# Six weight blocks kept on chip, an earlier load in the v task, other PSUM tiles for two gate blocks, and 384 tokens in token layout

## The chip, the cores and the metric

One core of a Trainium2 chip runs the whole kernel. The metric is the device time of one execution in microseconds (us); lower is better. The core has TensorE (PE, matmuls and transposes into PSUM), VectorE (DVE), ScalarE (ACT), GpSimd (POOL) and SyncE (SP). SP and ACT issue the DMAs. PEld in the profile is PE's weight loading, and a name with q behind it (SPq, ACTq) is an engine's instruction queue.

## The reference

One inference step through two layers for 1024 prompt tokens and 32 sample tokens, width 1024, all in float32.

```python
# layer 0 (even): a | u v | gate = rms_norm(x) @ w_in (1024 x 5120)
y_a = pool_mixer(a, ...)                 # trailing means 2/4/8/16 minus a, per-group linear, scale
u, v = gelu(uv);  v = layer_norm(v)      # for the sample tokens v is an output (state_sgu_v_sample)
y_b = u * (W_s v + b)                    # chunks of 128 positions, 4 heads, chunk-causal
x = x + rms_norm((concat(y_a, y_b) * silu(gate)) @ w_out)
# layer 1 (odd): q_c (384) | kv_c (256) | k_r (64) | gate (1024) = rms_norm(x) @ w_in_odd
q = rms_norm(q_c) @ w_q_up;  ckv = rms_norm(kv_c);  k_rope, q_rope = rope(...)
o = softmax(mask((q_abs . ckv + q_rope . k_rope) * scale)) @ ckv      # 8 heads
x = x + rms_norm((o @ w_kv_up_v * silu(gate)) @ w_o)
```

Outputs are x of both groups, the pool and v states, and the key caches.

## The kernel before, in words

Activations lie transposed, 128 channels by 1056 tokens (1024 prompt, 32 sample). Tokens are cut in part "a" (columns 0 to 639, two matmuls of 320) and part "b" (640 to 1055, one of 416). Every float32 operand is split in a high and a low half (`float32r`), and a product is three matmuls: high x high, high x low, low x high. `prep_w` (L140) fetches a weight block of 128 x 1024 in two halves of 512 columns: a DMA on SP into `raw` (three buffers), a cast on ACT to `whi` (four buffers), and the difference on POOL, or on DVE where `lo_on` says so, to `wlo` (four buffers). `mm_block` (L164) multiplies one block.

PE's instructions stand in the order in which the program writes them. A small planner writes them: `mm` adds each matmul's estimated time to a clock `now`, `spawn` puts a task (a Python generator) in a list with a due time, `poll` after each k step lets one due task write its next piece, and each `yield` says how long to wait, from the table `N` (ns). `drain` writes out all that is left. The instructions of DVE, ACT, POOL and the DMA queues are put in order by the compiler, which may move an instruction ahead of others where its inputs are there, by its own estimate; on the chip each engine then keeps that order. The compiler also adds the waits, and a tile's place is taken over when the last user of the tile before it is done.

Layer 0 (`even`, L319): blocks 8 and 9 (u) are accumulated while x arrives, "a" in the PSUM tiles `zt[0]` and `zt[1]`, "b" in the two halves (two banks) of `zt[2]`. Then come the gate blocks 32 and 33, part by part, and `evac` (L188) multiplies each result by the norm. `t_prep` (L374) makes sums and differences of x; with them 14 pairs of blocks run as seven products each (`pair_block`, L468) in the three tiles of `zt` by turns, their weights loaded by `s_load` (L424) and split by `s_prep` (L446, L447). Pairs 0 to 3 are v. `v_task` (L540) transposes each on PE and writes it to DRAM (`vd`); after pair 3 `lead_task` (L510) reads `vd` back by 128 tokens in nine steps, into R(15) and R(12) by turns, takes mean and variance (L518 to L522), normalises (L523) and writes `vnd`. For the 32 sample tokens it applies gain and shift in two halves and writes the output.

Between the layers `residual` (L863) adds x and the normed output, for "a" and "b", splits the new x for layer 1 (L895, L896), and sums the squares for the next norm (L907); `rstd` (L200) makes the norm's row from such a sum: L209 on PE, L216 to L219, L227, then L240.

Layer 1: `odd_in` (L911) multiplies w2. Its first six blocks run for "a", then again for "b", because the norm of "b" comes later; `seq` lists them twice and `prep_w` fetches them each time. Eight gate blocks follow for "ab". Attention (L1032) writes `ogd`. The last product (`output`, L1277) is cut by tokens: the first 2 x OA columns, here 800, in eight blocks with the weights stationary (matmuls of 400, tag "za" of PSUM, here `sc`), the other 256 in token layout, two tiles of 128 tokens with the tokens stationary and 512 output channels moving (`tile_k`, L1339). `turn` (L1326) transposes these tokens' x. `final_a` (L1372) norms and writes the first part while the token tiles run: two DVE instructions per block (L1385, L1386). Each token tile ends with squares on ACT (L1361), the product with the gain (L1362), the power on POOL (L1366), L1369 and the write. PSUM has here two `sc` tiles of two banks and four `pj` banks, and "zb" and "mi" stand for `pj`.

Of the kernel before, what the change touches and what calls it, by code (L numbers as in the profile page):

```python
# [24 lines left out]
OA = 400  # L25
# [9 lines left out]
N = {"ld0": 18000, "ld": 8500, "tp": 5500, "sa": 9000, "sl": 12000, "sb": 6000, "sbk": 2000, "sg": 0, "x": 462, "mix": 3200, "mixq": 2450, "tr": 717, "lead": 9000, "tr0": 11989, "res": 9194, "ra": 2699,  # L35
# [41 lines left out]
class Build:  # L77
# [62 lines left out]
    def prep_w(self, src, n=1024, lo_on=None, pool=None):  # L140
# [3 lines left out]
        for o in range(0, n, 512):  # L144
            m = min(512, n - o)
            raw = self.t(self.stg, [P, 512], F32, "raw", bufs=RAW)
            hi = self.t(pool or self.stg, [P, 512], F32R, "whi", bufs=4)
            lo = self.t(pool or self.stg, [P, 512], F32R, "wlo", bufs=4)
            nc.sync.dma_start(raw[:, :m], src[:, o : o + m])
            nc.scalar.copy(hi[:, :m], raw[:, :m])  # L150
            (lo_on or nc.gpsimd).tensor_tensor(lo[:, :m], raw[:, :m], hi[:, :m], ALU.subtract)  # L151
            res.append((hi, lo))
# [166 lines left out]
    def even(self):  # L319
# [91 lines left out]
        wts[33] = self.prep_w(self.i_w1[33], lo_on=nc.vector)  # L411
# [75 lines left out]
        for g, z in (("a", zz), ("b", z)):  # L487
# [5 lines left out]
            for i in range(2):  # L493
                ps = (zt[i], None) if g == "a" else (None, zt[2][:, i, :])
# [15 lines left out]
        def lead_task():  # L510

            for t in range(9):
                n = P if t < 8 else 32
                v = R(12 if t % 2 else 15)[:n, :D]
                nc.sync.dma_start(v, vd[t, :n])
                bs = self.t(evc, [P, 2, 6], F32, "bs", bufs=2)
# [8 lines left out]
                if t == 8:  # L525
                    w = R(13)
                    for e in range(2):
                        lg, lnb = w[:32, :512], w[:32, 512:1024]
                        o = slice(e * 512, e * 512 + 512)
                        nc.sync.dma_start(lg, self.i_lnbc[:, o])  # L530
                        nc.sync.dma_start(lnb, self.i_lnbc[:, D + e * 512 : D + e * 512 + 512])
                        nc.vector.tensor_tensor(lg, lg, v[:, o], ALU.mult)
                        nc.vector.tensor_tensor(lg, lg, lnb, ALU.add)
                        nc.scalar.dma_start(self.o_sv[:, o], lg)
# [26 lines left out]
        for p, (b0, b1) in enumerate(pairs):  # L561
# [6 lines left out]
            if p < 4:  # L568
                self.spawn(v_task(p, d), N["tr0"])
# [293 lines left out]
    def residual(self, g, acc, y):  # L863
# [47 lines left out]
    def odd_in(self):  # L911
        nc = self.nc
        h2 = self.h2
        wts = {0: self.prep_w(self.i_w2[0])}
        seq = list(range(6)) * 2 + list(range(6, 14))
        z = self.yp[:6]

        def block(i, groups, ps=None):
            w = wts.pop(i)
            if i + 1 < len(seq):  # L920
                wts[i + 1] = self.prep_w(self.i_w2[seq[i + 1]])
            return self.mm_block(self.wcol(w), h2, range(NK), groups, ps=ps)
# [3 lines left out]
        for b in range(6):  # L926
            pss.append(block(b, "a"))
# [12 lines left out]
        pss = [block(6 + b, "b", (None, zs[b])) for b in range(4)]  # L940
        self.drain()
        for b in range(6):
            self.evac(pss[b] if b < 4 else block(6 + b, "b"), z[b], rep2, "b")
# [73 lines left out]
        for m in range(8):  # L1017
            ps = block(12 + m, "ab")
# [258 lines left out]
    def output(self, w2, z2):  # L1277
# [59 lines left out]
        z = [self.bank("za") for _ in range(nt)]  # L1337

        def tile_k(j, k):  # L1339
            xh, xl = (v.b[:, j * P : (j + 1) * P] for v in og[k])  # L1340
            for c in range(2):
                hi, lo = wr[k][c]
                for e, (xx, w) in enumerate(((xh, hi), (xh, lo), (xl, hi))):
                    self.mm(z[j][:, c, :], xx, w, k == 0 and e == 0, k == NK - 1 and e == 2, 512)
# [7 lines left out]
        for j in range(nt):  # L1352
# [6 lines left out]
            for c in range(2):  # L1359
                junk = self.t(tp, [P, na], F32, "a", bufs=2)  # L1360
                nc.scalar.activation(junk[:, :512], z[j][:, c, :], AF.Square, accum_out=st[:, c : c + 1])  # L1361
            nc.vector.tensor_tensor(yg.rearrange("p (c n) -> p c n", c=2), z[j],  # L1362
                                    gb.rearrange("p (c n) -> p c n", c=2), ALU.mult)
# [124 lines left out]
```

## Time and profile before

| | |
|---|---|
| median of 3 runs | 1305.01 us (1299.88, 1305.31, 1305.01) |
| the profiled execution | 1299.84 us, span 1298.0 us |
| mean granted PE clock | 0.991 of full speed |
| busy: PE, DVE, ACT, POOL | 1255.4, 862.1, 552.5, 306.4 us |
| HBM read and written | 101.74 and 36.21 MB |

The page shows busy times, the chain of work that ended last, and groups of instructions by line. The waits view names for each idle time the engine, the line that waited, and what released it. A row of the windows view gives a stretch, the busy us of PE, PEld, DVE, ACT and POOL with their instruction counts, then the granted clock, the DMA share and GB/s. A timeline row is start, duration, engine, line, operation, output <- input, shape and count; in brackets stands the idle time before it and what ended that. Some 28 us of PE's span are idle by the timeline, the last 13.94 us aside.

### The profile page before, as it was taken

To read this page: it belongs to the slowest core of one execution; us is meant where nothing else is said; L and a number is where in the kernel's file an instruction comes from. 1 tells how busy PE (TensorE), PEld (TensorE's weight loads), DVE (VectorE), ACT (ScalarE), POOL (GpSimd) and SP (SyncE) were. 2 spreads that over 40 slices of the span, in tenths; PEclk is the share of its full clock that TensorE was granted. 3 is DMA by queue.
4 is the path that set the end of the run, shared out by engine and by line. 5 is a ranking of instruction groups with operands and counts; after the bars stand their busy time and mean duration, and the time that the engine had idled before them with its cause. 6 is when DMAs were issued, how large, how long until landed. Compare 5 with 4: busy or idle time off the path is not lost.

```text
span 1298.0 us, 22126 instructions
## 1 busy us (share of the span) xinstructions
PE 1255.4 (97%) x8488; PEld 1222.3 (94%) x8488; DVE 862.1 (66%) x1616; ACT 552.5 (43%) x1039; POOL 306.4 (24%) x381
## 2 busy tenths in 40 slices
PE   9899999999999999999999899999999999999995
PEld 8899999999999999999998899998999999998994
DVE  7977668886768764478487925634667666665438
ACT  8643432343423223243354423425566565654431
POOL 0200000000033433553002454223223332322510
PEclk9899999999999999999999999999999999999998
DMA  6023346522233245232455333322111111126425
GB/s 229 17 83 100 100 155 224 191 67 85 95 110 108 72 152 164 69 102 66 139 182 172 125 106 103 106 87 75 31 45 42 49 47 52 49 57 199 156 87 199
DMA packets 77562, 139.40 MB, mean 107 GB/s; under 512 B 10736, under 2 KB 33712, under 8 KB 77456
## 3 DMA queue, kind: packets, MB, share of 16 engines
q1 hardware_dynamic: 57776, 105.57, 26.3%
q10 hardware_dynamic: 19680, 32.42, 6.9%
q8 instruction: 67, 1.10, 0.4%
q14 instruction: 39, 0.32, 0.1%
HBM read 101.74 MB, written 36.21 MB: 106 GB/s over the span
## 4 chain that ended last, share of the span: by engine, by line
PE 79%; DVE 11%; DMA 4%; issue 3%; ACT 2%; POOL 1%; ACTq 0%; SPq 0%; DVEq 0%; POOLq 0%
PE za L115 20%; PE z L115 18%; PE sc L115 12%; PE pj L115 11%; PE zb L115 11%; PE pj L1162 2%; PE mi L115 2%; DMA r<-vd 1%; DVE wlo L447 1%; DVE wlo L151 1%; PE mi L209 1%; PE mi L549 1%; DVE r L907 1%; DVE a L1385 1%; DVE l L884 1%
## 5 line engine op out<-in xcount | busy, mean ns | idle before, releaser
L115 PE MATMUL z<-l,whi 128*128 128x264 f32 (+2 forms) x1312 | 247.5, 294 | 7.3 <-DVE r L192 2.1
L150 ACT CAST whi<-raw 128x512 fp32r<-128x512 f32 (+1 forms) x180 | 107.9, 603 | 290.1 <-PE zb L115 121.2
L151 POOL TENSOR_TENSOR wlo<-raw,whi 128x512 fp32r<-128x512 f32 (+2 forms) x122 | 157.8, 1296 | 289.0 <-ACT whi L150 285.4
L115 PEld LDWEIGHTS z<-l,whi 128*128 128x128 f32 x1312 | 196.2, 190 | 10.6 <-ACT r L378 2.4
L115 PE MATMUL z<-l,wlo 128*128 128x264 f32 (+2 forms) x880 | 187.1, 291 | 3.3 <-DVE wlo L447 3.3
L115 PE MATMUL za<-a,whi 128*128 128x320 f32 x704 | 144.2, 312 | 0.9 <-DVE r L641 0.9
L115 PEld LDWEIGHTS z<-l,wlo 128*128 128x128 f32 x880 | 139.1, 190 | 4.0 <-DVE wlo L447 3.9
L115 PEld LDWEIGHTS za<-a,whi 128*128 128x128 f32 x704 | 116.1, 188 | 1.5 <-ACT whi L150 1.2
L115 PE MATMUL za<-l,whi 128*128 128x320 f32 (+1 forms) x496 | 111.7, 315 | 0.0
L1135 POOL TENSOR_SCALAR p<-p,nm 128x128 f32<-128x128 f32 (+8 forms) x72 | 52.7, 732 | 164.2 <-DVE nm L1134 132.2
L115 PEld LDWEIGHTS za<-l,whi 128*128 128x128 f32 x496 | 90.4, 190 | 0.7
L115 PE MATMUL z<-r,whi 128*128 128x264 f32 x448 | 90.8, 284 | 0.0
L115 PE MATMUL za<-a,wlo 128*128 128x320 f32 x352 | 80.2, 309 | 0.0
L115 PE MATMUL zb<-l,whi 128*128 128x416 f32 x224 | 76.5, 353 | 0.0
L115 PE MATMUL zb<-b,whi 128*128 128x416 f32 x224 | 71.3, 353 | 0.0
L1133 ACT ACTIVATE p<-sc,nm 128x128 f32<-128x128 f32 (+8 forms) x72 | 50.5, 702 | 44.9 <-DVE nm L1132 33.8
L115 PEld LDWEIGHTS z<-r,whi 128*128 128x128 f32 x448 | 69.2, 188 | 0.0
L446 ACT CAST whi<-r 128x512 fp32r<-128x512 f32 x56 | 34.5, 620 | 76.2 <-PE z L115 60.2
L115 PEld LDWEIGHTS za<-a,wlo 128*128 128x128 f32 x352 | 61.5, 188 | 0.2
L447 DVE TENSOR_TENSOR wlo<-r,whi 128x512 fp32r<-128x512 f32 x56 | 38.3, 685 | 30.5 <-ACT whi L446 30.4
L115 PE MATMUL sc<-a,whi 128*128 128x400 f32 x256 | 57.7, 346 | 0.2 <-ACT p L1133 0.2
L115 PE MATMUL za<-l,wlo 128*128 128x320 f32 (+1 forms) x248 | 57.8, 312 | 0.0
(319 smaller groups left out, 3035.4 us busy)
## 6 DMA issues: line engine op xcount, KB each, us to landing
raw<-in_w SPq DMA_DIRECT2D x64, 256.0 KB, 2.7
r<-in_w SPq DMA_DIRECT2D x56, 256.0 KB, 2.8
raw<-in_wout SPq DMA_DIRECT2D x56, 256.0 KB, 3.0
mBd<-r ACTq DMA_DIRECT2D x8, 528.0 KB, 2.8
gAd<-r ACTq DMA_DIRECT2D x8, 528.0 KB, 3.5
l<-mBd SPq DMA_DIRECT2D x8, 528.0 KB, 6.3
vd<-r ACTq DMA_DIRECT2D x16, 256.0 KB, 2.8
r<-vd SPq DMA_DIRECT2D x8, 512.0 KB, 4.9
```

The lines of the kernel that those rows point to most:

```text
L115: self.nc.tensor.matmul(out, lhsT, rhs, start=start, stop=stop)
L150: nc.scalar.copy(hi[:, :m], raw[:, :m])
L151: (lo_on or nc.gpsimd).tensor_tensor(lo[:, :m], raw[:, :m], hi[:, :m], ALU.subtract)
L209: nc.tensor.matmul(st[:w, j : j + 1], acc[:, j * P : j * P + w], self.one, start=True, stop=True)
L446: nc.scalar.copy(hi, src)
L447: lo_on.tensor_tensor(lo, src, hi, ALU.subtract)
L549: nc.tensor.transpose(pt[:n, j * 256 + e * P : j * 256 + (e + 1) * P], d[e][:, i * P : i * P + n], self.ident)
L884: nc.vector.scalar_tensor_tensor(yy, yy, self.vec(GP1, m), rep, ALU.mult, ALU.mult)
L907: nc.vector.tensor_tensor(acc2, acc2, sq, ALU.add)
L1133: nc.scalar.activation(pv, view, AF.Exp, bias=nm[:n, 0:1], accum_out=nm[:n, 1:2])
L1135: nc.gpsimd.tensor_scalar(p[:n, :K], p[:n, :K], nm[:n, 2:3], 1.0, ALU.mult, ALU.mult)
L1162: nc.tensor.transpose(tr[:, e, :], p[:, (b + e) * P : (b + e + 1) * P], self.ident)
```

## The change

- `prep_w` can write to places given by the caller (`into`). `odd_in` fetches the six blocks once: blocks 0 and 1 stay in the four rotating `whi`/`wlo` buffers, blocks 2 and 3 go to R(5) to R(8), blocks 4 and 5 to the "a" tiles 0 to 7 of `rb`. `residual` for "b" packs its work tiles two by two in R(0) to R(4).
- `lead_task` issues the load of tile t + 1 ahead of the work on tile t, and the gain and shift of the last tile at step 7 into R(13) and R(14), whole. It starts its first load at 12000 and its work 8500 later, where it was 18000 for both; the last `v_task` is due 5000 after its pair, not 11989.
- Gate blocks 32 and 33 of "b" use `zt[0]` and `zt[2]`, first halves, and not the two halves of `zt[2]`. Block 33's low halves are made on POOL, not on DVE.
- `OA` is 336: 672 columns with weights stationary, 384 tokens in three token tiles. The third one takes two `pj` banks. The product with the gain is done by halves.

```diff
-OA = 400
+OA = 336
-N = {"ld0": 18000, ...
+N = {"ld0": 12000, ...
-    def prep_w(self, src, n=1024, lo_on=None, pool=None):
+    def prep_w(self, src, n=1024, lo_on=None, pool=None, into=None):
...
+            if into is None:
+                hi = ...whi, bufs=4;  lo = ...wlo, bufs=4
+            else:
+                hi, lo = into[o // 512]
...
-        wts[33] = self.prep_w(self.i_w1[33], lo_on=nc.vector)
+        wts[33] = self.prep_w(self.i_w1[33])
...
-                ps = (zt[i], None) if g == "a" else (None, zt[2][:, i, :])
+                ps = (zt[i], None) if g == "a" else (None, zt[2 * i][:, 0, :])
...
-            for t in range(9):
+            def load(t):
                 n = P if t < 8 else 32
                 v = R(12 if t % 2 else 15)[:n, :D]
                 nc.sync.dma_start(v, vd[t, :n])
+                return v
+
+            nxt = load(0)
+            yield N["ld"]
+            for t in range(9):
+                n = P if t < 8 else 32
+                v = nxt
+                if t < 8:
+                    nxt = load(t + 1)
+                if t == 7:
+                    lg, lnb = (R(i)[:32, :D] for i in (13, 14))
+                    nc.sync.dma_start(lg, self.i_lnbc[:, :D])
+                    nc.sync.dma_start(lnb, self.i_lnbc[:, D:])
...
-                    for e in range(2):
-                        (load lg and lnb by halves into R(13), multiply, add, write)
+                    nc.vector.tensor_tensor(lg, lg, v, ALU.mult)
+                    nc.vector.tensor_tensor(lg, lg, lnb, ALU.add)
+                    nc.scalar.dma_start(self.o_sv, lg)
...
-                self.spawn(v_task(p, d), N["tr0"])
+                self.spawn(v_task(p, d), N["tr0"] if p < 3 else 5000)
...
-            rep, acc2, *sq2 = (R(i)[:, :n] for i in range(9))
+            rep, acc2, *sq2 = (v for i in range(5) for v in (lambda o: (o[:, :n], o[:, HT : HT + n]))(R(i)))
...
-        seq = list(range(6)) * 2 + list(range(6, 14))
-        def block(i, groups, ps=None):
-            w = wts.pop(i)
-            if i + 1 < len(seq):
-                wts[i + 1] = self.prep_w(self.i_w2[seq[i + 1]])
-            return self.mm_block(self.wcol(w), h2, range(NK), groups, ps=ps)
+        def place(b):
+            if b < 2 or b > 5:
+                return None
+            if b < 4:
+                r = [self.R(5 + 2 * (b - 2) + h, F32R) for h in range(2)]
+                return [(v[:, :512], v[:, 512:1024]) for v in r]
+            r = [self.ab(self.rb, 4 * (b - 4) + h, F32R, "a").a[:, :512] for h in range(4)]
+            return [r[:2], r[2:]]
+
+        def block(b, groups, ps=None, ahead=False):
+            if ahead and b + 1 < 14:
+                wts[b + 1] = self.prep_w(self.i_w2[b + 1], into=place(b + 1))
+            return self.mm_block(self.wcol(wts[b]), h2, range(NK), groups, ps=ps)
...
-        z = [self.bank("za") for _ in range(nt)]
+        z = []
+        for j in range(nt):
+            v = self.bank("za") if j < 2 else None
+            z.append([v[:, c, :] if j < 2 else self.bank("zb") for c in range(2)])
...
-            nc.vector.tensor_tensor(yg.rearrange("p (c n) -> p c n", c=2), z[j],
-                                    gb.rearrange("p (c n) -> p c n", c=2), ALU.mult)
+            for c in range(2):
+                v = slice(c * 512, (c + 1) * 512)
+                nc.vector.tensor_tensor(yg[:, v], z[j][c], gb[:, v], ALU.mult)
```

In `odd_in` the next block is fetched ahead in blocks 0 to 4 of "a", in block 5 of "b" and in the gate blocks.

More of the change, by code (lines that the diff above doesn't have):

```diff
@@ L146, in prep_w @@
             raw = self.t(self.stg, [P, 512], F32, "raw", bufs=RAW)
-            hi = self.t(pool or self.stg, [P, 512], F32R, "whi", bufs=4)
-            lo = self.t(pool or self.stg, [P, 512], F32R, "wlo", bufs=4)
+            if into is None:
+                hi = self.t(pool or self.stg, [P, 512], F32R, "whi", bufs=4)
+                lo = self.t(pool or self.stg, [P, 512], F32R, "wlo", bufs=4)
+            else:
+                hi, lo = into[o // 512]
             nc.sync.dma_start(raw[:, :m], src[:, o : o + m])
@@ L525, in lead_task @@
                 if t == 8:
-                    w = R(13)
-                    for e in range(2):
[L528 to L534, printed above, removed]
+                    nc.vector.tensor_tensor(lg, lg, v, ALU.mult)
+                    nc.vector.tensor_tensor(lg, lg, lnb, ALU.add)
+                    nc.scalar.dma_start(self.o_sv, lg)
                 yield N["ld"]
@@ L914, in odd_in @@
         wts = {0: self.prep_w(self.i_w2[0])}
-        seq = list(range(6)) * 2 + list(range(6, 14))
         z = self.yp[:6]
-        def block(i, groups, ps=None):
-            w = wts.pop(i)
-            if i + 1 < len(seq):
-                wts[i + 1] = self.prep_w(self.i_w2[seq[i + 1]])
-            return self.mm_block(self.wcol(w), h2, range(NK), groups, ps=ps)
+        def place(b):
[10 more added lines that the diff above has]
+            return self.mm_block(self.wcol(wts[b]), h2, range(NK), groups, ps=ps)
         pss = []
         for b in range(6):
-            pss.append(block(b, "a"))
+            pss.append(block(b, "a", ahead=b < 5))
             if b == 0:
@@ L939, in odd_in @@
         zs = [self.bank("zb"), self.bank("zb"), za[:, 0, :], za[:, 1, :]]
-        pss = [block(6 + b, "b", (None, zs[b])) for b in range(4)]
+        pss = [block(b, "b", (None, zs[b])) for b in range(4)]
         self.drain()
         for b in range(6):
-            self.evac(pss[b] if b < 4 else block(6 + b, "b"), z[b], rep2, "b")
+            self.evac(pss[b] if b < 4 else block(b, "b", ahead=b == 5), z[b], rep2, "b")
         self.shut(self.rb)
@@ L1017, in odd_in @@
         for m in range(8):
-            ps = block(12 + m, "ab")
+            ps = block(6 + m, "ab", ahead=True)
             gt = self.yp[6 + m % 2]
@@ L1343, in tile_k @@
                 for e, (xx, w) in enumerate(((xh, hi), (xh, lo), (xl, hi))):
-                    self.mm(z[j][:, c, :], xx, w, k == 0 and e == 0, k == NK - 1 and e == 2, 512)
+                    self.mm(z[j][c], xx, w, k == 0 and e == 0, k == NK - 1 and e == 2, 512)
                 self.poll()
```

4 lines of the change are left out of this document (2 added, 2 removed).

## The prediction

> **What bounds the kernel now.** I read the page first (busy shares, then the chain that ended last), then what TensorE (PE) waited for, then PE's busy time and granted clock in stretches around its longest waits, and last the timeline of the engine named in each wait.
>
> ```profile
> PE 1255.4 (97%) x8488; PEld 1222.3 (94%) x8488; DVE 862.1 (66%) x1616; ACT 552.5 (43%) x1039; POOL 306.4 (24%) x381
> ...
> PE 79%; DVE 11%; DMA 4%; issue 3%; ACT 2%; POOL 1%; ACTq 0%; SPq 0%; DVEq 0%; POOLq 0%
> ```
>
> PE is busy 97% of the span and carries 79% of the chain. An edit that leaves the matmuls alone can therefore win only PE's waits, the time in which its clock is low, and the end, where PE has finished. The waits by releaser (total us, times, longest):
>
> ```profile
> PE mi L209 <- DVE r L907: 5.2, 1, 5.2
> PE z L115 <- DVE wlo L447: 3.3, 3, 1.8
> PE z L115 <- DVE r L192: 2.1, 1, 2.1
> PE z L115 <- DVE r L194: 2.0, 1, 2.0
> PE z L115 <- DVE r L480: 1.6, 2, 1.1
> ```
>
> Each of these lies in a place that the change touches: L192 and L194 in the gate blocks, L447 and L480 beside the v task, L907 in the w2 stage. Next the stretches (PE, PEld, DVE, ACT, POOL busy us, then the granted clock):
>
> ```profile
> 36.20:39.00 2.80, 2.80 (x18) 2.77 (x19) 1.40 (x4) 2.77 (x5) 0.69 (x1) 0.78 0.04 12
> 39.00:42.00 3.00, 3.00 (x15) 3.00 (x14) 2.98 (x9) 3.00 (x4) 2.79 (x5) 0.63 0.02 5
> ...
> 60.50:62.00 1.50, 1.49 (x7) 1.47 (x8) 1.50 (x3) 1.50 (x2) 0.00 (x0) 0.89 0.00 0
> 62.00:66.00 4.00, 4.00 (x16) 3.88 (x15) 3.37 (x5) 2.31 (x5) 0.00 (x0) 0.61 0.19 66
> ...
> 186.00:192.00 6.00, 3.37 (x25) 2.97 (x25) 5.80 (x12) 1.33 (x3) 0.56 (x1) 1.00 0.18 69
> ...
> 741.20:746.40 5.20, 0.01 (x1) 0.00 (x0) 4.99 (x6) 0.62 (x1) 3.13 (x3) 0.80 0.72 237
> 746.40:749.00 2.60, 2.59 (x12) 2.56 (x13) 0.90 (x3) 0.74 (x1) 0.68 (x1) 0.50 0.87 305
> 749.00:752.00 3.00, 3.00 (x15) 3.00 (x15) 1.64 (x5) 0.00 (x0) 1.23 (x6) 0.64 0.04 15
> ...
> 1255.18:1284.06 28.88, 27.66 (x135) 21.82 (x134) 21.74 (x40) 9.74 (x18) 2.89 (x6) 1.00 0.38 121
> 1284.06:1298.00 13.94, 0.00 (x0) 0.00 (x0) 10.50 (x16) 1.26 (x4) 1.07 (x2) 0.61 0.74 292
> ```
>
> A wait costs more than its length. Behind the 2.1 us wait the clock is 0.78, then 0.63: 0.22 x 2.8 + 0.37 x 3.0 = 1.7 us lost. Behind the 2.0 us wait 0.11 x 1.5 + 0.39 x 4.0 = 1.7 us; behind the 5.2 us wait 0.50 x 2.6 + 0.36 x 3.0 = 2.4 us. Behind the 1.8 us wait at 186 us the clock stayed at 1.00. In the last 13.94 us PE does nothing at all.
>
> **The gate blocks.** Block 32 and block 33 of part "b" share one PSUM tile, and the second waited until the first one's result had been read:
>
> ```profile
> 33.40 1.88 DVE L151 TENSOR_TENSOR wlo<-raw,whi 128x512 fp32r<-128x512 f32 x3
> 35.21 1.54 DVE L192 TENSOR_TENSOR r<-z,rep 128x640 f32<-128x640 f32 x2
> ...
> 59.87 0.58 DVE L194 TENSOR_TENSOR r<-z,rep 128x416 f32<-128x416 f32 x1
> ...
> 60.51 0.65 PE L115 MATMUL z<-l,whi 128*128 128x416 f32 x2 [1.96 <-DVE r L194]
> ...
> 66.91 0.59 DVE L194 TENSOR_TENSOR r<-z,rep 128x416 f32<-128x416 f32 x1 [1.50 <-PE z L115]
> ```
>
> The two halves are different banks, and block 33's was not the one being read, so the wait comes from the shared tile. With two tiles it goes: -2.0 and the clock's -1.7, -3.7 us. DVE must then have its operands for the second product that much sooner. It idled 1.50 us ahead of L194 at 66.91, waiting for PE itself, so it moves along; I give 0.5 back (ends: 0 and 1.5, that idle time). Next late are the splits of the last quarter of x.
>
> The low halves of block 33 move from DVE to POOL. One of the three L151 instructions ahead of L192 is among them, 1.88 / 3 = 0.6 us: the 2.1 us wait becomes 1.5, below the 1.8 that left the clock alone. Ends: -0.6 - 1.7 = -2.3, and +1.2 (POOL holds DVE up twice, by the difference of 0.6 that the w2 rows below show between a 1.3 us low half on POOL and one of 0.7 on DVE). I take -1.0, as I cannot place the POOL instructions. Together -4.2 us, between -6.0 and -1.0 (-3.7 + 1.5 + 1.2). If the copies on DVE are not the cover I take them for, L192 remains the wait.
>
> [...]
>
> **The v task.** v is read back by tiles in two buffers, and DVE waited for the first one:
>
> ```profile
> 186.12 1.29 DVE L518 BATCH_NORM_STATS2 bs<-r 128x6 f32<-128x512 f32 x2 [7.09 <-DMA r<-vd]
> ...
> 188.05 0.51 PE L115 MATMUL z<-l,wlo 128*128 128x264 f32 x2 [1.81 <-DVE wlo L447]
> ...
> 269.78 0.49 PE L115 MATMUL z<-l,whi 128*128 128x264 f32 x2 [1.14 <-DVE r L480]
> ```
>
> The low half that PE needed at 188 us stood behind that instruction on DVE. The change writes the last quarter of v 7.0 us of planner time sooner (5000 for 11989), issues each load one tile earlier, and fetches the gain and shift of the last tile ahead, in two transfers in place of four, with two DVE pairs merged into one (same elements). But a load still needs its buffer, which is free only when the tile before has been written out; so SP may stand at it with the weight loads for the next products behind it. What is at stake are PE's waits on L447 and L480, 3.3 + 1.6 = 4.9 us. Ends: -4.9, and +2 (the same load late again, now ahead of another product, 1.8). I take -2.0: the 1.14 beside the end of the task and half of the first wait.
>
> **The weights of w2.** Six blocks are multiplied twice (columns 0 to 639, then the rest) and were fetched and split twice. Now once: 12 loads on SP, 12 casts on ACT and 12 low halves on POOL go, and blocks 2 to 5 have places of their own in place of the four rotating ones. What they cost shows ahead of the 5.2 us wait; the first row is the second pass, in which PE had no gap:
>
> ```profile
> 756.50:784.20 27.70, 27.70 (x147) 27.26 (x147) 4.85 (x8) 8.06 (x14) 16.98 (x13) 1.00 0.33 105
> ...
> 735.64 0.64 DVE L896 SCALAR_TENSOR_TENSOR b<-l,vecs,b 128x416 fp32r<-128x416 f32 x1
> ...
> 737.50 1.20 DVE L907 TENSOR_TENSOR r<-r,r 128x416 f32<-128x416 f32 x2
> 738.62 1.69 DVE L896 SCALAR_TENSOR_TENSOR b<-l,vecs,b 128x416 fp32r<-128x416 f32 x1
> 740.23 6.13 DVE L907 TENSOR_TENSOR r<-r,r 128x416 f32<-128x416 f32 x5
> ...
> 738.27 4.75 POOL L151 TENSOR_TENSOR wlo<-raw,whi 128x512 fp32r<-128x512 f32 x3 [6.76 <-ACT whi L150]
> 743.27 1.32 POOL L151 TENSOR_TENSOR wlo<-raw,whi 128x512 fp32r<-128x512 f32 x1 [0.25 <-ACT whi L150]
> ```
>
> While POOL makes low halves, the same L896 takes 1.69 instead of 0.64, and five L907 take 6.13 instead of 5 x 0.6 = 3.0. The two together lose 1.05 + 3.1 = 4.2 us, on the very chain for which PE waits. Of the four POOL instructions the last two belong to the second pass and go (about 1 us each), and the first two are block 5's, which stood there because their place came free late; with places of their own they can run sooner. If all four leave, L907 ends some 4.2 us sooner and the wait shrinks from 5.2 to 1.0, too short for the clock to fall: -4.2 - 2.4 = -6.6. With only the last two gone, the wait is about 3 us and the clock's loss stays: -2. Ends: -7.6 (wait and clock wholly) and -1 (the earlier low halves hold DVE up in the norm ahead of it, and half of the 2 is lost). I take -6.0. SP's loads and ACT's casts that went ran beside PE and are worth nothing themselves.
>
> **The end: 384 tokens in token layout.** Eight blocks of 48 matmuls shrink from 400 to 336 columns; 48 matmuls of 512 and two groups of four transposes are added.
>
> ```profile
> 707.99 1.76 PE za L115 x12
> ...
> 1200.00:1255.18 55.18, 55.18 (x306) 55.18 (x304) 19.43 (x23) 18.28 (x31) 19.34 (x14) 1.00 0.40 125
> ...
> 1257.41 0.44 PE pj L1331 x4
> 1257.85 2.09 PE sc L115 x9
> ```
>
> A 400 column matmul is 55.18 / 306 = 180 ns, one of 320 is 1.76 / 12 = 147; 336 lies at 153.5, so 384 x 26.8 ns = -10.3. One of 512 is 2.09 / 9 = 232 ns: 48 x 232 = +11.1, and 2 x 0.44 = +0.9. PE does 1.7 us more. The gain is behind it:
>
> ```profile
> 1274.21 2.01 DVE L1385 SCALAR_TENSOR_TENSOR a<-a,vecs,repa 128x800 f32<-128x800 f32 x2
> ...
> 1287.33 1.88 DVE L1386 TENSOR_TENSOR a<-a,rawa 128x800 f32<-128x800 f32 x2
> ...
> 1291.68 1.07 POOL L1366 TENSOR_TENSOR sm<-sm,mhalf 128x1 f32<-128x1 f32 x2 [25.37 <-DVE sm L1364]
> ...
> 1292.28 2.74 DVE L1369 SCALAR_TENSOR_TENSOR yg<-yg,sm,xt 128x512 f32<-128x512 f32 x4 [0.42 <-POOL sm L1366]
> ```
>
> DVE runs 16 instructions of final_a from 1274.2 to 1289.2, 5 us past PE's end, and both token tiles stand behind them. At 672 columns the 16 take about 15 x 0.85 = 12.7 us. They start 19 us into the token stage, so they end at 32; PE then works 28.9 + 11.1 + 0.9 = 40.9 us in it. DVE is free 9 us before PE ends and only the third tile remains: ACT's two squares (its 1.26 of the last stretch), two small sums of some 0.2, the power 1.07 / 2, two L1369 of 2.74 / 4, and 1298.0 - 1295.0 = 3.0 for the last write: 6.6, with a hand-over 6.7 us, in place of 13.9, -7.2. Net -5.5 us. Ends: -7.2 (the 1.7 hidden in today's small waits), and -3 (the third tile's turn on DVE, ACT and SP costs what a tile costs between L1385's end and the last L1369 now, 5.8 / 2 = 2.9, on top).
>
> **Sum.** -4.2 - 2.0 - 6.0 - 5.5 = -17.7. The compiler plans the order of DVE, ACT, POOL and SP anew, and the load of the sixth and seventh ogd blocks loses up to 1.9 us of matmul cover (72 matmuls, 26.8 ns each); for both +2: -15.7. The profiled execution took 1299.8 us, so 1284.1. Of the runs shown one stands there and two 5.3 us above, with the median at 1305.0; I add half of that, 2.6: **1287 us**.
>
> [...]
>
> **Rivals.**
> *The lock moves.* Low halves made sooner hold DVE up in the norms ahead of the chain instead. For: POOL's instructions of blocks 2 to 5 all remain. Against: two of the four go for certain. The w2 part then gives 1, not 6: 1292.
> *The first half gives nothing.* What the gate blocks win is lost behind the v loads. For: DVE works 5.80 of the 6 us from 186 us, so it catches up slowly. Against: it stood idle for 7.09 just before. 6.2 us less, 1293.
> *No change that can be told.* Both at once, 11.2 us less, leave -4.5, 1298; with the third tile at its worse end, +2.5, 1300.
> *Slower.* The third token tile holds two of the four pj banks to the end, and the six groups of transposes, two norm rows and one sum, nine in all, must share the other two. Each hand-over that PE waits for costs its wait and perhaps the clock. It decides from a mean of (15.7 + 6.5) / 9 = 2.5 us each. Against: of the 28.88 us of this stage PE works 27.66 now, with seven of these and four banks. At 3 us each: 1314.
>
> **Chances.** Half a per cent, 6.5 us, is about what a measurement of this kernel can tell from no change. Forecast 0.54; the lock moves 0.17; first half nothing 0.14; no change 0.10; slower 0.05. Faster 0.85, same 0.10, slower 0.05. Range: the good ends of all parts (-6.0 - 4.9 - 7.6 - 7.2 = -25.7) give 1274 on the profiled time; nearer 8 in 10 is 1277, and up to 1299 it takes in the first two rivals and most of the third. The forecast's own range is 1280 to 1292.
>
> **What would show it.** Right: no wait on L194 near 58 us and a clock of 1.00 behind it; no 7 us wait of L518; L907 at 0.6 us each and a wait below 2 us ahead of L209, clock 1.00 after; PE's last matmul 6 to 7 us before the span's end, with final_a's last L1386 well ahead of it. Wrong: L907 stretched as now; PE waiting on pj in the token stage; L518 waiting again; new waits of 2 us with a low clock behind.

## The result, and the profile after

| | before | after |
|---|---|---|
| median of 4 runs each, side by side | 1305.16 us (1299.88 to 1306.36) | 1287.13 us (1284.31 to 1290.67) |
| profiled execution, span | 1299.84, 1298.0 us | 1286.02, 1284.2 us |

The ratio is 0.9871, 95% interval 0.9834 to 0.9908: 17 us less. The changed kernel's line numbers are a little higher (L192, L194, L896 and L907 are now L195, L197, L906 and L917; L1331 and L1366 are L1349 and L1388; L1385 and L1386 are L1407 and L1408).

The page of the changed kernel, its busy shares and its chain:

```profile
PE 1255.4 (98%) x8542; PEld 1220.8 (95%) x8542; DVE 854.3 (67%) x1618; ACT 547.9 (43%) x1033; POOL 287.3 (22%) x372
...
PE 71%; DVE 4%; DMA 2%; issue 1%; ACT 1%; POOL 1%; SPq 0%; DVEq 0%; POOLq 0%; ACTq 0%
```

Among what PE waited for in the changed kernel (total us, times, longest):

```profile
PE mi L115 <- DVE dgl L230: 2.1, 1, 2.1
PE mi L115 <- DVE dgh L230: 1.8, 1, 1.8
PE z L115 <- DVE r L195: 1.5, 1, 1.5
PE sc L115 <- ACT whi L153: 1.4, 1, 1.4
```

PE is busy as long as before. The waits on L194, L447 and L907 are gone. In their place stand two on the diagonal tiles of a norm (L230), one of which was 1.0 before, and one on a weight's high half. The stretches, in the same columns as before:

```profile
39.00:42.00 3.00, 3.00 (x22) 3.00 (x21) 2.13 (x5) 2.86 (x5) 2.50 (x7) 1.00 0.02 5
...
699.60:712.00 12.40, 12.36 (x73) 11.87 (x74) 4.24 (x12) 3.72 (x6) 9.60 (x12) 0.86 0.55 167
729.00:740.00 11.00, 11.00 (x79) 10.97 (x78) 6.66 (x16) 0.39 (x1) 1.93 (x6) 1.00 0.03 12
...
1233.37:1276.64 43.27, 41.10 (x190) 32.68 (x188) 28.88 (x54) 12.71 (x26) 3.37 (x8) 0.96 0.42 144
1276.64:1284.20 7.56, 0.00 (x0) 0.00 (x0) 3.77 (x8) 0.78 (x4) 0.54 (x1) 0.79 0.36 139
```

From 39 to 42 us the clock is full, where it was 0.63. Ahead of the norm's column sums (729 to 740) PE does not stop. The tail is 7.56 us, not 13.94. New is a clock of 0.86 behind 699.60, where PE has waited 2.1 us: one of the signs that the prediction gave for being wrong.

To tell the parts apart I cut every trace at the same five matmuls, and at the end of the last one. PE's timeline rows of the five in the changed kernel are v's first transpose, then the starts of the pool stage, the scores, the w_o blocks and the tiles in token layout:

```profile
98.63 0.60 PE L559 MATMUL mi<-ident,r 128*128 128x128 f32 x4
453.04 0.46 PE L115 MATMUL za<-r,whi 128*128 128x320 f32 x2
876.80 0.33 PE L115 MATMUL sc<-knh,qnh 128*128 128x128 f32 x1 [0.91 <-ACT qnh L1089]
1168.72 0.89 PE L115 MATMUL sc<-a,whi 128*128 128x336 f32 x4 [0.22 <-ACT p L1151]
1233.37 0.40 PE L115 MATMUL sc<-whi,b 128*128 128x512 f32 x1
```

There are fourteen traces: before, after and the twelve runs below. "Without" is the mean over those that lack the part of the change in that stage, "with" over those that have it; runs with half of a part, or with another edit in that stage, are in neither. The range is in brackets. All are us.

| stage | without | with | difference | predicted |
|---|---|---|---|---|
| start to v's first transpose (gates) | 101.1 (99.1 to 103.0) | 99.2 (98.5 to 100.1) | -1.9 | -4.2 |
| to the pool stage (v task) | 360.9 (360.3 to 362.0) | 354.2 (353.6 to 355.1) | -6.6 | -2.0 |
| to the first scores (w2) | 430.4 (428.7 to 432.0) | 424.0 (422.9 to 424.5) | -6.4 | -6.0 |
| attention (not touched) | 291.1 (289.2 to 292.6) | 290.9 (289.0 to 291.9) | 0 | 0 |
| w_o blocks "a" | 75.2 (75.1 to 75.2) | 64.6 (64.6 to 64.7) | -10.5 | -10.3 |
| token stage | 28.9 (28.8 to 28.9) | 41.9 (41.0 to 43.3) | +13.0 | +12.0 |
| tail behind PE | 14.3 (13.9 to 14.6) | 8.0 (7.6 to 8.2) | -6.3 | -7.2 |

The sum is -18.7; the prediction's terms make -17.7. The two profiled executions alone differ by 13.8, because the one before lies at the short end in w2 (428.7) and attention (289.3); the reason stands at the end.

### The profile page after: what moved, and what is told of

It reads as the page before. It is cut to its first block, busy times and chain, and to the rows that moved or that the text cites. A ratio compares the mean times of both kernels' runs of the same rounds, so it can differ in the third digit from the quotient of the medians.

```text
span 1284.2 us, 22174 instructions
## 1 busy us (share of the span) xinstructions
PE 1255.4 (98%) x8542; PEld 1220.8 (95%) x8542; DVE 854.3 (67%) x1618; ACT 547.9 (43%) x1033; POOL 287.3 (22%) x372
## 4 chain that ended last, share of the span: by engine, by line
PE 71%; DVE 4%; DMA 2%; issue 1%; ACT 1%; POOL 1%; SPq 0%; DVEq 0%; POOLq 0%; ACTq 0%
PE za L115 22%; PE pj L115 13%; PE sc L115 12%; PE zb L115 12%; PE z L115 8%; PE pj L1180 2%; PE mi L115 2%; DVE wlo L154 1%; PE mi L212 0%; DMA raw<-in_wout 0%; DMA rawa<-x1d 0%; DMA gated<-l 0%; DMA rawa<-ogd 0%; DMA raw<-in_wok 0%; DMA r<-in_w 0%
## 5 line engine op out<-in xcount | busy, mean ns | idle before, releaser
L153 ACT CAST whi<-raw 128x512 fp32r<-128x512 f32 (+2 forms) x160 | 96.0, 601 | 263.0 <-PE zb L115 125.2
L154 POOL TENSOR_TENSOR wlo<-raw,whi 128x512 fp32r<-128x512 f32 (+2 forms) x104 | 133.0, 1281 | 264.9 <-ACT whi L153 218.0
L115 PE MATMUL za<-a,whi 128*128 128x320 f32 x640 | 132.7, 313 | 0.9 <-DVE r L651 0.9
L115 PEld LDWEIGHTS za<-a,whi 128*128 128x128 f32 x640 | 106.4, 189 | 1.5 <-ACT whi L153 1.2
L115 PE MATMUL za<-l,whi 128*128 128x320 f32 x416 | 94.7, 312 | 0.0
L115 PEld LDWEIGHTS za<-l,whi 128*128 128x128 f32 x416 | 77.1, 189 | 0.6
L115 PE MATMUL za<-a,wlo 128*128 128x320 f32 x320 | 73.1, 310 | 0.0
L115 PEld LDWEIGHTS za<-a,wlo 128*128 128x128 f32 x320 | 56.4, 189 | 0.2
L1183 DVE TENSOR_TENSOR pl<-pj,ph 128x512 fp32r<-128x512 f32 (+2 forms) x96 | 51.0, 552 | 7.1 <-ACT ph L1182 6.3
L154 DVE TENSOR_TENSOR wlo<-raw,whi 128x512 fp32r<-128x512 f32 x56 | 38.4, 690 | 23.6 <-ACT whi L153 23.6
```

The costliest lines, as they stand in the source:

```text
L115: self.nc.tensor.matmul(out, lhsT, rhs, start=start, stop=stop)
L1183: nc.vector.tensor_tensor(lo[:, :nb, off : off + P], tr[:, :nb, :], hi[:, :nb, off : off + P], ALU.subtract)
```

## The experiments

**Each part alone.** The end: `OA = 336`, the third tile's banks and the halves of the product, on the kernel before.

> The kernel before with the last part of the change alone: OA 336, so 384 last tokens in token layout, with the third tile's sums in two pj banks and the halves multiplied by gb one by one. The w2 weights, the gate blocks' PSUM tiles and the v task are as before. The whole change's profile has the eight 'a' blocks 10.8 us shorter, the stage of the last tokens 14.4 longer and the stretch from TensorE's last matmul to the end of the span 6.4 shorter. Theory (the parts are independent): the same three terms here, so the time is 2.8 us below before (0.2%); the stage of the last tokens shows the 1.4 us wait of TensorE for a weight's high half (ACT L150) that the changed kernel has near 1264. The prediction's terms would give -4.7. Rival (the end earns more, because the tail's cost was what the median hid, or the gains elsewhere are smaller than the landmarks say): 8 us or more below before. Rival on the other side (the third tile holds two of the four pj banks and the drain waits for them): 5 us or more above before, with waits of TensorE on pj in the last 45 us.

Measured: ratio 0.9963 (0.9948 to 0.9978), -4.8 us, nearer to the prediction's -4.7 than to the -2.8 read off the two profiles; stages -10.5, +12.2, -5.9. Its token stage and tail:

```profile
1246.71:1287.75 41.04, 39.52 (x190) 31.51 (x188) 28.40 (x53) 12.74 (x26) 3.31 (x8) 1.00 0.45 153
1287.75:1295.80 8.05, 0.00 (x0) 0.00 (x0) 4.24 (x8) 0.79 (x4) 0.60 (x2) 0.63 0.34 130
```

PE's longest wait there:

```profile
PE sc L115 <- ACT whi L150: 0.8, 1, 0.8
```

The wait on the high half belongs to this part, but it is 0.8 here, and the clock does not fall; in the whole change it was 1.4 and the stage 2.2 us longer. No wait on the third tile's pj banks: the slower rival is out.

The w2 weights: `place`, `block` and the packed work tiles of `residual`, on the kernel before.

> The kernel before with only the w2 weights kept: blocks 0 to 5 are loaded and split once, and the second pass over them reads the kept halves. Theory (POOL's low halves of the second pass hold up VectorE's row work, which the matmul of the norm waits for): PE's stretch from the pool stage's last wait (za on r, 684.56 in the kernel before) to the first scores of the attention falls from 206.2 us to about 200.5 (-5.4 to -6.0), the six L896-line squares sums at the end of the residual take 0.6 us each instead of up to 1.3, and the total is 5 to 6 us below before. Rival (the lock moves to the norms of the rows ahead, because the same twelve low halves now run earlier): the stretch falls by 2 us or less, with a new wait of TensorE over 3 us between 690 and 710 on the POOL-held diagonal tiles.

Measured: 0.9968 (0.9955 to 0.9981), -4.2 us, where 5 to 6 were expected. The stretch of the expectation is 200.2, -6.0. The wait of 5.2 is gone, and one appears in the norm ahead of it:

```profile
PE mi L115 <- DVE dgl L230: 2.1, 1, 2.1
```

So the hold did move, in small: 2.1 us where the wait was 1.04 in the kernel before. (The sums of the expectation are those of L907, not L896.)

POOL or the loads? On the kernel before, only the engine of the second pass's low halves:

```diff
-wts[i + 1] = self.prep_w(self.i_w2[seq[i + 1]])
+wts[i + 1] = self.prep_w(self.i_w2[seq[i + 1]], lo_on=nc.vector if 6 <= i + 1 < 12 else None)
```

> The kernel before with one argument changed: the twelve low halves of the second pass over w2 blocks 0 to 5 are subtracted on VectorE instead of POOL; loads, high halves, their buffers and every other step are as before, so each block is still loaded twice. Theory (it is POOL's work beside VectorE's that cost the time, not the loads or the splits as such): VectorE takes on 12 x 0.69 us, about 8 us, next to a stretched 5.2 + 3 us that goes; the wait for the residual's sums in front of the norm's column sums falls by at least half, and the stretch from 684.56 to the attention's first scores is 3 to 5 us shorter than 206.2. Rival A (the gain of the kept weights is the load and the ACT copies saved, which fill SP's queue and ACT): no gain here, the stretch within 1 us of 206.2. Rival B (VectorE is itself what is late there, and 8 us more in its queue ahead of the sums is worse than POOL's hold): the stretch 2 us or more longer.

Measured: 0.9997 (0.9983 to 1.0012); the stretch is 204.4, -1.8. The timeline of DVE, and PE's row behind it:

```profile
735.63 1.69 DVE L896 SCALAR_TENSOR_TENSOR b<-l,vecs,b 128x416 fp32r<-128x416 f32 x1
737.25 2.92 DVE L907 TENSOR_TENSOR r<-r,r 128x416 f32<-128x416 f32 x3
740.08 0.68 DVE L151 TENSOR_TENSOR wlo<-raw,whi 128x512 fp32r<-128x512 f32 x1
740.68 1.21 DVE L907 TENSOR_TENSOR r<-r,r 128x416 f32<-128x416 f32 x2
...
741.95 1.64 PE L209 MATMUL mi<-one,r 128*128 128x1 f32 x8 [3.72 <-DVE r L907]
```

The last two L907 take 0.6 each, with a low half of 0.68 on DVE between them. Beside block 5's two low halves, which POOL still makes, L896 takes 1.69 and one L907 takes 1.67; the other two of the three take 0.59. In the kernel before, the trace has four such instructions beside POOL's four low halves (1.69, 1.67, 1.54 and 1.53), and the rest take 0.6: the mean of 1.2 in the prediction's row is three held and two free.

The wait falls from 5.2 to 3.7, not by half, and the total shows nothing. This is the prediction's case "with only the last two gone": a wait of about 3 and a gain of 2 were worked out, 3.7 and 1.8 came. So the result lies between theory and rival A: the hold is real, and this edit removes the second pass's share of it. That the other share needs block 5's earlier place is not shown by a run of its own; with kept weights no sum is held.

The gate blocks: `zt[2 * i][:, 0, :]` and block 33's low halves on POOL, on the kernel before.

> The kernel before with the gate part alone: the last token group of gate block 33 goes to PSUM tile zt[2] instead of the half that shares a bank with block 32's, and block 33's low halves are subtracted on POOL instead of VectorE. Theory (prediction's term): the 2.2 us wait on block 32's eviction near 58 us and the 0.6 to 0.7 clock behind it go, the first wait near 35 falls from 2.12 to about 1.5, granted clock 1.00 over 50 to 100 us where before has 0.97; total 4.2 us below before. Rival (the sum in the first half belongs to the v task): 1 us or less below before, with a new wait in place of the old one by 70 us.

Measured: 0.9993 (0.9978 to 1.0008), -0.9 us; 98.9 to v's first transpose, -2.1 against the kernel before. Blocks 32 and 33 each had a half of `zt[2]` (L322, 2 x 512 columns), so what they shared was the tile; that they shared a bank, as the expectation has it, is not shown. Block 32 now goes to `zt[0]`, block 33 to the first half of `zt[2]`. The waits did what was said (L192 1.5, L194 gone, 2.0 before), and a wait of 0.9 on x's last splits came instead. The size was wrong.

**The v task in two.** The load ahead alone, on the kernel before:

> The kernel before with the load of v one tile ahead alone (each of the nine tiles is loaded a step before it is used, the two rows of lnbc once and whole); the fourth v task keeps its due time of 11989 and the norm's task its 18000. In the kernel before TensorE waits 6.2 us in all between 150 and 300 us, for split weights and sums that stand behind VectorE; in the whole change it waits nowhere over 0.3 there, and the stretch from the first transpose of v to the pool stage falls from 361.0 us to 354.4 (-6.6, where the prediction had -2.0). Theory A (VectorE's queue was held by bn_stats waiting up to 7.1 us for the tile's load, and the splits behind it were late): the load ahead takes that wait away by itself, the stretch is 355.5 or less. Theory B (the early due time is what counts: the last transposes come 8 us sooner, so the written v is there when it is read): here the stretch stays within 1.5 us of 361, with a load of v that still waits for its write near 190 us and a wait of VectorE on it of 4 us or more.

The due times alone:

> The kernel before with the due times alone: the fourth v task due 5000 after its pair instead of 11989, the norm's task 12000 instead of 18000; v is loaded in the step that uses it, as before. Theory A (load ahead is the cause): VectorE's bn_stats still waits for each tile's load, 2 us or more each in one or two places, and the stretch from the first transpose of v to the pool stage stays above 358.5 (361.0 in the kernel before, 354.4 in the whole change). Theory B (due time is the cause): the stretch falls to 356 or less and the 7.1 us wait on the load is 3 us or less.

Both together, the whole v part:

> The kernel before with the whole v part alone: v loaded one tile ahead, lnbc's rows once, the fourth v task due 5000 and the norm's task 12000. The load ahead alone made the stretch from v's first transpose to the pool stage 5.7 us shorter (361.0 to 355.3), the due times alone 3.4. Theory (both act on the same waits of TensorE, 6.2 us in 150 to 300, and do not add): 354 to 355, no wait of TensorE over 0.5 us between 150 and 300, no granted clock below 1.00 there, and the total 5 to 7 us below before. Rival (what the stretch gives is handed back in the w2 and attention stages, as the load ahead alone ended only 2 us below before): the stretch is 354 to 355 and the total within 3 us of before.

| v's first transpose to pool stage | us | ratio to before |
|---|---|---|
| load ahead alone | 355.3 | 0.9985 (0.9974 to 0.9997) |
| due times alone | 357.7 | 1.0004 (0.9989 to 1.0020) |
| both | 355.1 | 0.9964 (0.9952 to 0.9976), -4.7 us |

PE's longest wait between 150 and 300 us with the load ahead alone:

```profile
PE z L115 <- DVE r L474: 1.2, 2, 0.8
```

With the due times alone:

```profile
PE z L115 <- ACT r L473: 1.1, 1, 1.1
```

With both, the longest is 0.4. And what DVE waited for with the load ahead alone:

```profile
DVE bs L531 <- DMA r<-vd: 6.7, 2, 5.7
```

By the stretch theory A holds: the load ahead brings nearly all of it, the due times half, and they overlap. But its mechanism is only half right. VectorE still waits 5.7 us for the first tile, whose due time this run leaves late; with both edits the longest such wait is 2.3. What goes are the waits inside the later tiles' steps, behind which weights and sums were late. That the load ahead alone ended only 2 us lower while its stretch is 5.7 shorter fits its trace, which has 432.0 in the w2 stage, the longest of all: the clock was at half for 3.4 us from 573 us, where the kernel before kept it, and for 10.2 us from 740, where the kernel before had 6.8. With both, the total follows the stretch to within 2 us, and at -4.7 it stays just short of the 5 to 7 expected.

The four parts alone make -4.8 - 4.2 - 0.9 - 4.7 = -14.6 us. The whole makes -16.8 (-21.7 to -12.0) of 1305; they add up within the intervals.

**POOL against DVE for block 33.** On the changed kernel:

```diff
-wts[33] = self.prep_w(self.i_w1[33])
+wts[33] = self.prep_w(self.i_w1[33], lo_on=nc.vector)
```

> The changed kernel with the two low halves of gate block 33 back on VectorE. Theory (the prediction's: VectorE's queue ahead of the first rows is what TensorE waits for near 35 us, and POOL took two subtractions out of it): the wait on r (L195) near 35 us is 2.1 again instead of 1.5, and TensorE's first matmul on a split quarter of x, at 66.2 in the changed kernel, comes 0.6 to 1.0 us later. [...]

Measured: 0.9882 (0.9853 to 0.9912), the same as the changed kernel's 0.9871. The wait near 35 is 2.1 again. The diagonal pair in the changed kernel's timeline:

```profile
39.87 1.72 DVE L230 TENSOR_SCALAR dgh<-ident,rh 128x128 fp32r<-128x128 f32 x2 [1.41 <-POOL rh L221]
```

In this one's:

```profile
40.72 0.51 DVE L230 TENSOR_SCALAR dgh<-ident,rh 128x128 fp32r<-128x128 f32 x2 [0.35 <-POOL rh L221]
```

And its two longest waits of PE up to 100 us:

```profile
PE z L115 <- DVE r L195: 2.1, 1, 2.1
PE z L115 <- DVE r L393: 1.3, 1, 1.3
```

The pair is held up beside POOL: 1.72 for 0.51. Whether that costs more than the move frees, this run can't decide. Its clock was at half from 37.7 to 44.5 us, two stretches of 3.4 us. PE reaches x's splits at 68.1; the changed kernel and its variants reach them at 66.2 to 66.6 with a full clock and at 67.6 to 67.7 with one such stretch, so two explain all of the 1.9. With the slow clock PE also comes late to the diagonal tiles, and the 1.8 us wait there does not show.

A better pair are two traces with a full clock in this stage: the changed kernel, and the run with only the second pass's low halves moved, which has block 33's on DVE. From the norm's copy (L243, L240) to the end of the second L195 or L192, DVE takes 14.33 us with POOL (33.39 to 47.72) and 13.77 without (32.77 to 46.54). So the move took 0.6 out ahead of the first product, and the hold put 1.2 in. PE's first wait is 1.5 for 2.1, its wait at the diagonal tiles 1.8 for 1.2: nothing gained. The 1.2 is the size that the prediction gave as the poorer end (as twice 0.6; here it is one hold). Its -1.0 for the move did not come.

**The hold in the first pass.** On the changed kernel, w2 blocks 1 and 2's low halves on DVE:

```diff
-into=place(b + 1))
+into=place(b + 1), lo_on=nc.vector if b < 2 else None)
```

> The changed kernel with the low halves of w2 blocks 1 and 2 subtracted on VectorE instead of POOL; all else as in the changed kernel. Theory (the same hold of POOL over VectorE that the change took out of the second pass is left in the first one: the diagonal tiles of L230 took 1.51 for two and 2.52 for two beside POOL's subtractions, and TensorE waited 2.06 at 697.54 and ran at 0.86 to 712): the L230 tiles take 0.55 a pair, the wait falls below 1 us, and the stretch from the pool stage to the attention's first scores falls by 2 to 3.5 us from 423.8. Rival (VectorE's 4 x 0.69 us stand in front of the diagonal tiles in its queue and wait there for loads and high halves): the wait is 2 us or more, and the stretch is the same or longer.

Measured: 0.9870 (0.9849 to 0.9892), no difference; 424.9 us in the stage. The L230 pairs at 693 to 697 us take 0.5 each and the wait at 697.5 is gone. Its place takes this one:

```profile
PE mi L115 <- DVE dgh L230: 2.1, 1, 2.1
```

The timeline of POOL, then of DVE:

```profile
706.13 1.30 POOL L154 TENSOR_TENSOR a<-raw,a 128x512 fp32r<-128x512 f32 x1 [0.28 <-ACT a L153]
707.38 1.36 POOL L220 TENSOR_TENSOR sm<-sm,mhalf 128x3 f32<-128x3 f32 x2
...
702.89 0.21 DVE L219 TENSOR_SCALAR sm<-mi 128x3 f32<-128x3 f32 x2 [2.26 <-PE mi L212]
708.91 0.52 DVE L230 TENSOR_SCALAR dgh<-ident,rh 128x128 fp32r<-128x128 f32 x2 [5.82 <-POOL rh L221]
```

The power of the next norm was ready to run at 703.1 and ran at 707.4, behind the low halves of blocks 4 and 5 in POOL's own queue. Neither theory named that: POOL's low halves held the L230 pairs up (1.51 and 2.52 us in the changed kernel, 0.5 here), and POOL is also a queue, in which the power stood 4.3 us.

**The load behind the writes.** On the changed kernel, `"fy": 648` becomes `"fy": 2000`.

> The changed kernel with the steps of the final norm's rows (L1407 to L1411) spaced 2000 apart by the planner instead of 648, so that more of the rows and of their writes on SP's queue come behind the load of the last w_o block in token layout. Theory (TensorE's 1.4 + 0.2 us wait near 1264 on the last high half, and the lower clock to 1270.8, come from that load standing behind writes that wait for VectorE): the load is issued by 1256, the wait is gone, the stage of the last tokens falls from 43.3 us to 40.5 or less, and the total by 2 to 3 us. Rival (the rows that come later now stand in front of the first tile's products with gb on VectorE): the stage shortens, but the stretch behind TensorE's last matmul grows by 1.5 us or more from 7.6, and the total stays within 1 us. Second rival (the load is late because of its raw buffer, which is free only when VectorE has done the low half before it): the wait stays, 1 us or more.

Measured: 1283.29 us (1282.84 to 1283.70), 0.9854 (0.9838 to 0.9870). In the changed kernel SP's last w_o load stood behind three writes that waited for DVE, ACT's high half waited for that load (ACT idled 8.19 us), and PE waited for the high half:

```profile
1257.84 2.93 SPq L1411 DMA_DIRECT2D out_yT<-a  x3
1260.86 0.38 SPq L152 DMA_DIRECT2D raw<-in_wok  x1
...
1264.71 0.62 ACT L153 CAST whi<-raw 128x512 fp32r<-128x512 f32 x1 [8.19 <-DMA raw<-in_wok]
...
1265.38 0.49 PE L115 MATMUL sc<-whi,b 128*128 128x512 f32 x1 [1.40 <-ACT whi L153]
```

With the rows spaced out, SP's load:

```profile
1254.24 0.43 SPq L152 DMA_DIRECT2D raw<-in_wok  x1
```

and the token stage and the tail:

```profile
1234.22:1273.68 39.46, 38.92 (x190) 31.59 (x188) 28.36 (x53) 12.62 (x26) 3.28 (x8) 1.00 0.46 158
1273.68:1281.90 8.22, 0.00 (x0) 0.00 (x0) 4.25 (x8) 0.78 (x4) 0.63 (x2) 0.63 0.33 128
```

The theory holds: the load goes 6.6 us sooner, the wait is gone, the clock is 1.00. The stage is 39.5 us, 1.6 to 3.8 less than in the traces with the wait; the tail is as in those (8.0 on average). The total is 2.2 us below the changed kernel by the ratios to the kernel before (0.9854 and 0.9871); their intervals overlap, so it is the stage that shows the gain.

**The order at the end.** On the changed kernel, the last tile's matmuls by column half, and only its first half written from ACT's queue:

```diff
-                tile_k(j, k)
+                tile_k(j, k, (0, 1) if j < nt - 1 else (0,))
+            if j == nt - 1:
+                for k in range(KS, NK):
+                    tile_k(j, k, (1,))
...
-(nc.sync if c else nc.scalar).dma_start(self.o_yL
+(nc.sync if c or j < nt - 1 else nc.scalar).dma_start(self.o_yL
```

> The changed kernel with the end of the last tiles reordered: the last tile's matmuls of k = 5 to 7 go by column half, first all of half 0, then all of half 1, and only the last tile's first half is written from ACT's queue, the other writes from SP's. Theory (the stretch behind TensorE's last matmul is a queue of the tiles before it: ACT's squares of the second tile start only when the write of the first tile ahead of them in its queue has its data, VectorE's products with gb follow the squares, and the third tile's follow those): the squares of the second tile start at their matmul's end, the last tile's products with gb start within 1 us of TensorE's last matmul, and the stretch to the end of the span falls from 7.6 us to 6.4 or less. Rival (the stretch is bound by what depends on the last matmul alone: squares, sum, power, row, write): it stays within 0.5 us of 7.6.

Measured: 0.9881 (0.9858 to 0.9904), a tail of 7.7. The theory falls. DVE's rows say why (PE's last matmul ended at 1274.83):

```profile
1273.63 0.69 DVE L1388 TENSOR_TENSOR yg<-pj,gb 128x512 f32<-128x512 f32 x1
1275.05 1.41 DVE L1394 SCALAR_TENSOR_TENSOR yg<-yg,sm,xt 128x512 f32<-128x512 f32 x2 [0.66 <-POOL sm L1391]
1276.38 0.68 DVE L1388 TENSOR_TENSOR yg<-pj,gb 128x512 f32<-128x512 f32 x1
```

The first half's product does move ahead of the last matmul. The second half's then stands behind the second tile's rows, which wait 0.66 for POOL's power: it starts 1.55 after PE's end.

Both edits of the end together:

> The changed kernel with both edits of its end: rows of the final norm spaced 2000 apart (measured alone: the stage of the last tokens 39.5 instead of 43.3 us, the stretch behind it 8.2 instead of 7.6), and the reordered end of the last tiles. Theory (both independent): the stage 39.5 us, the stretch behind it 6.6 to 7.0, so a median of 1282 us, 1.5 to 2 us below the kernel with the spaced rows alone at 1283.3. Rival (the write queue of SP, which now holds the writes of the rows and of two tiles, is late at the end): the stretch stays at 8 us, and the time is the same as that of the spaced rows.

Measured: 1284.04 us (1283.18 to 1285.29), 0.9851 (0.9828 to 0.9874); token stage 39.4, tail 7.7. The stage holds; the tail gains 0.5 where 1.2 or more was expected, too little to see in the total. The spaced rows are the version to keep.

## Why the prediction was right

The time, 1287 for 1287.1, is right, and the parts pay in the places that were named. That it agrees to 0.1 us is luck. By the stage means the v task is off by -4.6, the gate blocks by +2.3, the end by +1.7 and w2 by -0.4, and this cancels to -1.0; the +2 allowed for the compiler was not needed, and the step from one profiled execution to the median was a guess of 2.6.

*v task: -6.6, not -2.0, and outside the ends given.* The mis-sized step is "what is at stake are PE's waits on L447 and L480, 3.3 + 1.6 = 4.9 us", of which 2.0 was taken. The same view has 0.8 (L474) and 0.4 (L477) more from the same late queue; that is 6.1, and as much went. The price of a late load there (+2) came at none of the tiles: the longest wait of bn_stats on a load is 2.3 us in the changed kernel, not 7.1.

*Gate blocks: -1.9, not -4.2.* The first wait became 1.5, as worked out, and L194's went. "I give 0.5 back" was too little: PE then waited 0.9 at x's splits, the place named as next late, and the -1.0 for POOL's low halves came back as 1.8 for 1.2 at the diagonal tiles. And the clock's 1.7 us behind each wait was counted as certain. It is not: the run with only the second pass's low halves moved has the gate waits of 2.1 and 2.0 us and full clock behind them.

```profile
PE z L115 <- DVE r L192: 2.1, 1, 2.1
PE z L115 <- DVE r L194: 2.0, 1, 2.0
```

The stretch behind the first; the one behind the second stands in the last section:

```profile
38.00:42.00 4.00, 4.00 (x29) 4.00 (x28) 3.47 (x10) 4.00 (x6) 3.79 (x5) 1.00 0.02 4
```

Most of the -1.9 is that clock. With no fall in the stage, the one trace without the part takes 99.05 us and the three with it 98.5 to 98.9. The clock fell for 13 stretches of 3.4 us in the seven traces without the part, for 3 in the six with it. A wait that goes takes a chance of a fall with it; that is what this part mostly earned.

*w2: -6.4, for -6.0.* Right in place, and near in size. DVE's six last sums in the changed kernel, where five took 6.13, and then the last diagonal pair that PE waited for:

```profile
730.17 3.79 DVE L917 TENSOR_TENSOR r<-r,r 128x416 f32<-128x416 f32 x6
...
697.02 2.52 DVE L230 TENSOR_SCALAR dgl<-ident,sm 128x128 fp32r<-128x128 f32 x2
```

0.63 each, and no wait behind them. The second row is the rival "the lock moves": a wait of 2.06 us that ends at 699.60, where it was 1.04, and the clock's 1.7 behind it. It took some 2.7 us. Counted from the stage's start the sums end 3.4 us sooner (280.9 for 284.3), less than the 4.2 worked out; that no wait at all is left is because PE comes 2.6 later (281.8 for 279.2). So between the two profiled executions the stage gains 2.6 at the norm and the 2.4 of clock behind it, some 5 in all; the -6.4 of the means holds other falls of the clock too.

*The end: -3.8, not -5.5.* The 336 column blocks are exact (-10.5 for -10.3). The token stage is +13.0 for +12.0. (By its own terms the poorer end, given as -3, is -5.5 + 2.9 = -2.6.) Its matmuls alone cost less than the term, 39.5 - 28.9 = +10.6 in the kernel with the spaced rows; the rest is the wait behind SP's writes, which the prediction did not look for, though it names SP among the queues. The tail was counted as what depends on the last tile alone (6.6 to 6.7); it is 8.0, because the second tile's rows and their wait for POOL lie between. final_a is done 13 us ahead of PE's end, where 9 were worked out.

*The allowances.* The load of the ogd blocks (L1290) has a wait of 0.35 that the kernel before has not, where up to 1.9 was allowed, and the w_o blocks still gain 10.5: nothing of the +2 was needed. From the stage means the changed kernel would be at 1301.8 - 18.7 + 1.8 (time over span) = 1284.9; the other 2.2 us to the median lie in runs without a trace and stay open.

## What to carry to other kernels

Sum all the waits that one late queue causes, whatever line each is named by; the reason they share is the term, not the longest row. When a low-priority queue (writes, splits on POOL) carries one instruction that the critical engine needs, look at what is issued ahead of it in that queue: spacing the rows of a finished result took a wait out for nothing here, while moving work between POOL and DVE moved the wait or gave too little to tell. To size a part of under 1%, cut the traces at fixed instructions, and look which of them have a fallen clock in the stretch: the total of the whole v part says that it is worth more than 2.0 (3.1 to 6.2), but not which edit brought it, and most of what the gate blocks seemed to win was the clock.

## What was not expected of the hardware

The clock behind short waits falls in these traces by a fixed amount, to half for 3.41 us or a multiple of it, and the wait's length does not tell whether. Windows of the run with the gate part alone, near 40 us:

```profile
38.00:42.00 4.00, 4.00 (x18) 4.00 (x19) 2.58 (x6) 3.99 (x7) 3.64 (x7) 0.57 0.02 4
```

of the changed kernel at the start of attention:

```profile
878.00:882.00 4.00, 3.63 (x11) 3.27 (x12) 2.18 (x6) 2.19 (x4) 0.00 (x0) 0.53 0.00 0
882.00:886.00 4.00, 4.00 (x18) 4.00 (x17) 0.98 (x4) 1.70 (x6) 0.38 (x1) 0.62 0.00 0
```

and of the kernel before at the same place:

```profile
892.00:896.00 4.00, 3.63 (x21) 3.49 (x22) 1.82 (x7) 2.39 (x6) 0.20 (x1) 1.00 0.00 0
```

0.43 x 4 = 1.7 us are lost in the first, 0.47 x 4 + 0.38 x 4 = 3.4 in the second, nothing in the third. Between 1.4 and 2.1 us the wait's length does not decide: at the start of attention the run with block 33 on DVE waited 1.14 + 0.71 and lost nothing, the spaced rows waited 0.57 + 0.88 and lost 3.4. The attention stage, untouched, so varies from 289.0 to 292.6 us, and this is most of what separates the two profiled executions from the stage means.

What decides in these traces is where the wait falls on a grid of time. They record the granted clock to the nanosecond: it is full or half, and within a trace its changes lie a whole number of 3.413 us apart, to within 3 ns, over the whole 1300 us. In the kernel before, half clock starts at 37.78, 61.67 and 744.34 us, 7 and 200 such steps apart. A step at half loses half of 3.413, the 1.7 us seen above. The grid does not start with the kernel: its first step begins 0.24 us into the span in the kernel before, 1.01 in the changed kernel and 0.75 in the run with only the second pass's low halves moved. The same 2.0 us wait in the gate blocks, cut along the grid, in the kernel before:

```profile
58.26:61.67 3.41, 1.45 (x8) 1.15 (x7) 3.41 (x7) 2.97 (x4) 0.00 (x0) 1.00 0.00 0
61.67:65.08 3.41, 3.41 (x12) 3.29 (x11) 3.38 (x5) 1.72 (x4) 0.00 (x0) 0.50 0.23 77
```

and in the run with only the second pass's low halves moved, where the wait is shared between two steps:

```profile
58.78:62.19 3.41, 2.09 (x11) 2.07 (x12) 3.41 (x7) 2.48 (x3) 0.00 (x0) 1.00 0.00 0
62.19:65.60 3.41, 3.41 (x23) 3.38 (x22) 3.38 (x6) 2.26 (x5) 0.00 (x0) 1.00 0.28 82
```

PE idles 57% of the step in the first and 39% in the second. In all fourteen traces up to PE's last matmul, every one of the 31 full-clock steps that PE idled for more than 53% of has a half-clock step behind it; of the 5088 with less than 35%, none has; of the 40 between, 8 have. So the same wait of 2 us cost clock in one trace and none in another, by where the grid lay; where PE idled for less than 1.2 us of a step (35%), no clock was lost.
